# Window sums on another engine, key copies from another memory, and one step moved ahead, in a two-block transformer kernel

## The chip, the cores and the metric

The program runs on one core of a Trainium2 chip. Its time is device microseconds per execution; lower is better. The engines named here are TensorE (matrix products and transposes, called PE in the profile), VectorE (DVE), ScalarE (ACT), GpSimd (POOL) and SyncE (SP, whose queue issues the DMAs).

## The reference, cut to what matters

Two blocks of depth 2 follow each other on 512 tokens of width 1024, all in float32. The parts that the change touches are the multiscale pooling in both layers of the first block, the keys of the first mixer of the second block, and the latents of its second mixer.

```python
# block 1, both layers: window means of 2, 4, 8, 16 tokens (one window per 96 channels)
c = cs[:, :, g]                                   # running sum over tokens
prev = jnp.pad(c, ((0, 0), (w, 0), (0, 0)))[:, :s]
outs.append((c - prev) / cnt - ug[:, :, g])
pooled = jnp.stack(outs, axis=2)                  # then a small product per group

# block 2, layer 0: differential attention, 4 heads, two maps per head; and window attention
logits = [einsum('bqhmd,bkhmd->bmhqk', q, k) * scale for k, _ in kv_parts]   # 512 + 256 keys
outs = [einsum('bhqk,bkhd->bqhd', p[:, 0] - lam * p[:, 1], v) ...]

# block 2, layer 1: latent attention; one roped key of 32 features is shared by 16 heads
qn, qr = mla_queries(p[..., :C_Q_LORA], q_norm_g, wq_b)      # norm of 384 latents, product
kn, kr, v = mla_keys_values(p[..., C_Q_LORA:], kv_norm_g, wkv_b)
kr = apply_axial_rope(kr[:, :, None, :], tab)[:, :, 0, :]
```

## The kernel before

A float32 value is held as a high part, rounded to the matrix engine's reduced form, and a low part, the difference. `split` makes them: ScalarE copies the high part, VectorE subtracts. A product then takes three matrix products (`mm3`, lines 136 to 138): high by high, high by low, low by high. Weights arrive by DMA on SyncE's queue into three buffers, and `wload` splits them into five pairs of buffers.

**What sets the order.** The program is written as one sequence of instructions, and a planner in the compiler puts them into each engine's queue: it takes what its own model says is ready, earlier program lines first, and an engine then works through its queue strictly in order. Buffers are rings: a tile of a pool with n buffers waits until an earlier one is released.

**Attention and its filler.** In both attention stages of interest `pipeline` runs a list of items in four steps (scores with the maximum; exponential and scaling; transposes; product with the values). The steps of one item lie some items apart. After each round a `Fill` object runs generators that hold the next projections, up to an allowance in nanoseconds per item; a generator yields a cost figure for each piece, and a yield of 0.0 lets it stop early where little of the allowance is left. `need` runs what is left of a generator before the first item that uses it.

**Pooling** (`pool_in`, lines 579 to 605). It is filler in the first block's attention stage. For each of three chunks of 128 channels there is a projection of 8 x 3 products into a PSUM tile, a ScalarE copy to `u`, and then two, three or four doubling steps on GpSimd, each a small copy of the first columns (line 591) and one or two shifted additions (line 593). Two scalings at the window's start (line 599), two combined multiply-adds (lines 600 and 601) and a split follow on VectorE and ScalarE.

**Stacked keys** (`twice`, lines 1060 to 1074). The differential attention has ten items for each of four heads: eight for the tokens (four tiles by two maps) and two for the context. While one head's items run, `proj_ab` for the next group is the filler: six token tiles of 24 products and a rope, after the fifth tile the transposes of tiles 0 to 3, after the sixth those of the two context tiles. Keys of two maps come out of one transpose, 64 partitions each. For each map a tile of 128 partitions holds the high and low parts on its own 64 partitions and the same values again on the other 64:

```python
for h, k in enumerate(dsts):
    own, other = slice(64 * h, 64 * h + 64), slice(64 - 64 * h, 128 - 64 * h)
    self.split(k[own, 0, c], k[own, 1, c], ps[own])
    self.copy(k[other, 0, c], ps[own])
    self.copy(k[other, 1, c], f32(k[own, 1, c]))
```

`ps` is one of two PSUM tiles with the tag "p" that the projections and the value products use too (for the first group, which runs ahead of the items, the tags are "p" and "T"). `stacked` (lines 1044 to 1058) does the queries in a similar way, without copies.

**Latents** (`mla_latents`, lines 1413 to 1455). It projects key and value latents (288 columns) for six token tiles, then query latents (384 columns) for four, each with a norm, transposes and a split. The shared roped key, 32 columns, is gathered in `krs`; six transposes (line 1450), two splits of 32 x 768 and four GpSimd copies (line 1454) put it into the keys of both head pairs. The PSUM ring "ps" is closed behind this function, and the attention stage opens its own pools in the same banks.

Of the kernel before, what the change touches and what calls it, by code (L numbers as in the profile page):

```python
# [17 lines left out]
ALU = mybir.AluOpType  # L18
# [14 lines left out]
def f32(ap):  # L33
    return ap.bitcast(F32)
# [5 lines left out]
class Fill:  # L40
# [28 lines left out]
    def drain(self):  # L69
        while self.gens:  # L70
            self._one()
# [7 lines left out]
class Net:  # L79
# [499 lines left out]
    def pool_in(self, l, hT, pooled):  # L579
        nc, I = self.nc, self.I  # L580
        for c in range(3):
            yield 0.0
            ps = self.psum("p")
            yield from self.projT_steps(ps, self.wload(I["w_pool"][l, c]), hT)
            new = lambda: self.t2.tile([P, 4, P], F32, name="t2")
            u = new()
            self.copy(u, ps.rearrange("p (b j) -> p b j", b=4))
            cur, keep = u, []
            for i, k in enumerate((1, 2, 4, 8)[: c + 2]):
                nxt = new()  # L590
                nc.gpsimd.tensor_copy(self.heads(nxt, k), self.heads(cur, k))
                for (d, s), (d0, _) in zip(self.shifts(nxt, cur, k), self.shifts(cur, cur, k)):
                    nc.gpsimd.tensor_tensor(d, d0, s, op=ALU.add)  # L593
                cur = nxt
                keep.append(nxt)
            t = new()
            pc = self.poolc[:, c]
            for i, s in enumerate(keep[-2:]):
                nc.vector.tensor_tensor(s[:, :, 0:4], s[:, :, 0:4], pc[:, i, 1:17].rearrange("p (b j) -> p b j", b=4), op=ALU.mult)
            nc.vector.scalar_tensor_tensor(t, keep[-2], pc[:, 0, 0:1], u, op0=ALU.mult, op1=ALU.subtract)  # L600
            nc.vector.scalar_tensor_tensor(t, keep[-1], pc[:, 1, 0:1], t, op0=ALU.mult, op1=ALU.add)
            tt = self.qk.tile([P, 2, 512], R, name="qk")
            self.split(tt[:, 0], tt[:, 1], t.rearrange("p b j -> p (b j)"))
            pooled.append(tt)
# [455 lines left out]
    def twice(self, tok, col, tiles, dsts, tag):  # L1060

        tiles = list(tiles)
        n = len(tiles) * P
        yield 0.0
        ps = self.psum(tag)[:, :n]
        for j, t in enumerate(tiles):
            self.nc.tensor.transpose(ps[:, j * P : (j + 1) * P], tok[:, t, col : col + P], self.ident)
            yield 109
        c = slice(tiles[0] * P, tiles[0] * P + n)
        for h, k in enumerate(dsts):  # L1070
            own, other = slice(64 * h, 64 * h + 64), slice(64 - 64 * h, 128 - 64 * h)
            self.split(k[own, 0, c], k[own, 1, c], ps[own])
            self.copy(k[other, 0, c], ps[own])
            self.copy(k[other, 1, c], f32(k[own, 1, c]))

    def scores(self, ps, q, k):

# [212 lines left out]
    def mix_ab(self, hT, lead):  # L1290
        nc, I = self.nc, self.I
        with ExitStack() as ctx:
            with ExitStack() as c2:
                self.ringctx.close()
                self.psum_pools(c2, S=2, T=2, p=2)
                self.open_xc()
                hT = hT + self.new_hC()
                rows = []

                def pre(t):  # L1300
                    if not rows:
                        rows.extend((self.mod_row(0, 1, 1), self.mod_col(0, 1, 0)))
                    self.prenorm(self.xc[t - 4], rows[0], hT, t, rows[1])

                self.late += [(4, lambda: pre(4)), (5, lambda: pre(5))]
                cp = self.pool(c2, "const2")
                self.consts2(cp)
                self.tables(cp, ("cos_ab", "sin_ab"), 64)
                self.work = self.pool(c2, "attn")
                self.qk = self.pool(c2, "qk", 5)  # L1310
                fill = Fill(1500.0)
                gs = [{} for _ in range(6)]
                drain(self.proj_ab(hT, 0, gs[0], ("p", "T", "T")))
                self.xcctx.close()
                back = self.spill_x()
                self.qk2 = self.pool(c2, "qk2")
                self.ptp = self.pool(c2, "PT", 3)
                oBp = self.pool(c2, "oB")
                oB = [oBp.tile([P, 6, P], F32, name=f"oB{h}") for h in range(4)]
                proj = [(i, self.proj_ab(hT, i, gs[i], ("p",))) for i in range(1, 6)]  # L1320
                items = []
                for h in range(4):
                    items += self.diff_items(h, gs[h], fill, oB[h], proj[h])
                n, oT = len(items), []
                items += self.window_items(gs[4], gs[5], fill, oB, oT, proj[4])
                self.pipeline(items, fill, [3000] * n + [5000] * 8 + [200] * (len(items) - n - 8), (0, 1, 4, 5))
                fill.drain()
            self.open_x(back)
            self.open_xc()
            self.open_ring()  # L1330
            hT = self.b2_out(ctx, 0, oT, I["ab_w_out_2"], self.x + self.xc, lead)
        return hT
# [80 lines left out]
    def mla_latents(self, hT, lat, kTs):  # L1413

        nc, I = self.nc, self.I
        work = self.work
        gq = work.tile([P, 384], F32, name="gq")
        nc.sync.dma_start(gq, I["mla_q_norm_g_2"].rearrange("e d -> (e d)").partition_broadcast(P))
        gk = work.tile([P, 256], F32, name="gk")
        nc.sync.dma_start(gk, I["mla_kv_norm_g_2"].rearrange("e d -> (e d)").partition_broadcast(P))  # L1420
        qlT = (lat.tile([P, 3, 512], R, name="qlhi"), lat.tile([P, 3, 512], R, name="qllo"))
        klT = (lat.tile([P, 2, 768], R, name="klhi"), lat.tile([P, 2, 768], R, name="kllo"))
        krs = work.tile([P, 6, 96], F32, name="krs")
        nc.gpsimd.memset(krs, 0.0)

        def norm_T(src, n, g, dst, t):
            r = self.rstd(src, n)
            tok = work.tile([P, 384], F32, name="lat", bufs=2)[:, :n]
            nc.vector.scalar_tensor_tensor(tok, src, r, g, op0=ALU.mult, op1=ALU.mult)

            def tr():
                ps = self.psum()[:, 0]
                for c in range(n // P):
                    nc.tensor.transpose(ps[:, c * P : (c + 1) * P], tok[:, c * P : (c + 1) * P], self.ident)
                q = slice(t * P, (t + 1) * P)
                self.split(dst[0][:, :, q], dst[1][:, :, q], ps[:, :n].rearrange("p (c q) -> p c q", c=n // P))

            return tr

        def kv_evac(t, ps):  # L1440
            nc.vector.tensor_copy(krs[:, t, 64:96], ps[:, 256:288])
            if t < 4:
                self.rope2(krs[:, t : t + 1, 64:96], self.tabs["cos_c"][:, t], self.tabs["sin_c"][:, t], 1, 32)
            return norm_T(ps[:, :256], 256, gk, klT, t)

        drain(self.tok_proj(hT, I["mla_w_kv_2"], (4, 5, 0, 1, 2, 3), 288, kv_evac, tags=("ps",)))
        drain(self.tok_proj(hT, I["mla_w_q_2"], range(4), 384, lambda t, ps: norm_T(ps, 384, gq, qlT, t), tags=("ps",)))
        ps = self.psum().rearrange("p a b -> p (a b)")
        for t in range(6):
            nc.tensor.transpose(ps[:96, t * P : (t + 1) * P], krs[:, t], self.ident)  # L1450
        for j in range(2):
            self.split(kTs[j][0][64:96, 0], kTs[j][1][64:96, 0], ps[64:96, :768])
            for i in range(2):
                nc.gpsimd.tensor_scalar(kTs[j][i][64:96, 1], f32(kTs[j][i][64:96, 0]), 1.0, 1.0, op0=ALU.mult, op1=ALU.mult)
        return qlT, klT

    def proj_mla(self, grp, pr, qlT, klT, kT, g, tags):
# [316 lines left out]
```

## Time and profile before

| what | value |
|---|---|
| median of three timed runs | 3585.54 us (3582.1 to 3585.82) |
| the profiled execution: its own time, its span | 3584.89 us, 3583.1 us |
| TensorE, products | 3472.2 us busy, 97% |
| TensorE, weight loads (beside products) | 2966.2 us, 83% |
| VectorE | 1945.1 us, 54% |
| ScalarE | 1367.2 us, 38% |
| GpSimd | 411.1 us, 11% |
| mean granted TensorE clock | 0.989 |

The span runs from the first to the last instruction. Busy products are pipelined, so the 97% says that TensorE is rarely without work, not that it runs at its best rate. In a timeline each row has the start and the length in microseconds, the engine, the line, the operation and its tiles; in brackets stands how long the engine was idle before it and what it waited for.

### The profile page before, as it was taken

The page shows a single profiled execution, that of the slowest core. Times are in us where ns is not written, and L with a number is a line of the kernel's source. Part 1 is how long each engine was busy: PE and PEld are TensorE (multiplying, and loading weights), DVE is VectorE, ACT ScalarE, POOL GpSimd, SP SyncE. Part 2 cuts the span into 40 slices and gives each one's busy share as a digit, 9 for nine tenths or more (in the row PEclk, how much of TensorE's full clock was granted, in tenths as well). Part 3 has the DMA queues.
Part 4 walks back from the last instruction along what each step waited for, and adds up shares of the span by engine and source line. Part 5 has one row for each costly group of instructions (what it writes and reads, how often), then busy time and mean ns, then how long its engine had stood idle before and what let it go on. Part 6 is the DMA issues. An engine that isn't in the chain of part 4 may idle for free.

```text
span 3583.1 us, 48034 instructions
## 1 busy us (share of the span) xinstructions
PE 3472.2 (97%) x19101; PEld 2966.2 (83%) x19101; DVE 1945.1 (54%) x3140; ACT 1367.2 (38%) x2462; POOL 411.1 (11%) x532
## 2 busy tenths in 40 slices
PE   8999999999999999999999989999999989999998
PEld 8877798888897778988878887888888879888887
DVE  4453357466544435566767777536663466743243
ACT  4332344332443324532345556332111356643222
POOL 0201111000102111200010113200000122220001
PEclk9999999999999999999999999999999999999999
DMA  4243334344322433354331112325442121022232
GB/s 129 83 129 94 100 113 141 106 144 135 104 80 79 135 94 124 119 170 149 124 115 40 36 36 90 130 89 168 133 134 102 46 80 33 26 88 89 89 102 86
DMA packets 110129, 364.01 MB, mean 102 GB/s; under 512 B 16616, under 2 KB 18208, under 8 KB 109904
## 3 DMA queue, kind: packets, MB, share of 16 engines
q1 hardware_dynamic: 109904, 360.94, 31.8%
q8 instruction: 150, 2.46, 0.3%
q14 instruction: 75, 0.61, 0.1%
HBM read 347.16 MB, written 13.73 MB: 101 GB/s over the span
## 4 chain that ended last, share of the span: by engine, by line
PE 85%; DVE 5%; ACT 4%; POOL 2%; DMA 2%; issue 2%; SPq 0%; POOLq 0%; ACTq 0%; DVEq 0%
PE ps L136 21%; PE ps L137 21%; PE ps L138 21%; PE p L136 4%; PE p L137 4%; PE p L138 4%; PE p L456 2%; PE T L440 2%; DVE wlo L112 1%; PE S L1079 1%; DMA adaw<-in_ada_w_dram 1%; PE S L136 1%; POOL t L593 1%; PE p L1133 1%; ACT whi L109 1%
## 5 line engine op out<-in xcount | busy, mean ns | idle before, releaser
L112 DVE TENSOR_TENSOR wlo<-raw,whi 128x1024 fp32r<-128x1024 f32 (+2 forms) x510 | 604.2, 1189 | 740.1 <-ACT whi L109 720.1
L109 ACT ACTIVATE whi<-raw 128x1024 fp32r<-128x1024 f32 (+2 forms) x510 | 518.4, 1019 | 1152.7 <-PE ps L137 715.8
L137 PE MATMUL ps<-hTlo,whi 128*128 128x512 f32 (+1 forms) x2048 | 758.2, 370 | 4.3 <-DVE hTlo L184 3.4
L136 PE MATMUL ps<-hThi,whi 128*128 128x512 f32 (+1 forms) x2048 | 758.2, 371 | 2.7 <-ACT hThi L109 1.4
L138 PE MATMUL ps<-hThi,wlo 128*128 128x512 f32 (+1 forms) x2048 | 757.2, 370 | 0.0
L136 PEld LDWEIGHTS ps<-hThi,whi 128*128 128x128 f32 x2048 | 386.4, 189 | 73.2 <-issue 3.5
L137 PEld LDWEIGHTS ps<-hTlo,whi 128*128 128x128 f32 x2048 | 387.1, 189 | 69.6 <-DVE hTlo L184 3.9
L138 PEld LDWEIGHTS ps<-hThi,wlo 128*128 128x128 f32 x2048 | 386.9, 189 | 65.8
L945 DVE SCALAR_TENSOR_TENSOR acc<-adaw,cs,acc 128x1024 f32<-128x1024 f32 x168 | 209.6, 1280 | 12.5 <-DMA adaw<-in_ada_w_dram 12.3
L136 PE MATMUL ps<-whi,a 128*128 128x512 f32 x440 | 170.8, 392 | 0.5 <-ACT a L109 0.5
L138 PE MATMUL ps<-whi,a 128*128 128x512 f32 x440 | 170.6, 390 | 0.0
L137 PE MATMUL ps<-wlo,a 128*128 128x512 f32 x440 | 170.6, 390 | 0.0
L136 PE MATMUL p<-whi,hThi 128*128 128x384 f32 x464 | 161.2, 348 | 5.8 <-ACT hThi L182 3.1
L137 PE MATMUL p<-wlo,hThi 128*128 128x384 f32 x464 | 157.4, 339 | 4.0 <-DVE wlo L112 4.0
L138 PE MATMUL p<-whi,hTlo 128*128 128x384 f32 x464 | 157.5, 340 | 1.1 <-DVE hTlo L112 1.1
L269 DVE TENSOR_TENSOR y<-y,ps 128x1024 f32<-128x1024 f32 x88 | 106.6, 1218 | 85.9 <-PE ps L138 85.6
L161 POOL TENSOR_SCALAR rstd<-ms 128x1 f32<-128x1 f32 x54 | 18.5, 343 | 1073.7 <-ACT junk L159 1059.5
L136 PE MATMUL ps<-whi,act 128*128 128x512 f32 x352 | 138.1, 394 | 0.0
L137 PE MATMUL ps<-wlo,act 128*128 128x512 f32 x352 | 137.4, 392 | 0.0
L138 PE MATMUL ps<-whi,act 128*128 128x512 f32 x352 | 136.2, 390 | 0.0
L430 POOL TENSOR_SCALAR g<-g,den 128x768 f32<-128x768 f32 (+3 forms) x88 | 72.7, 828 | 478.0 <-DVE den L426 414.9
L409 DVE TENSOR_REDUCE nm<-S 128x1 f32<-128x768 f32 x96 | 91.4, 952 | 30.4 <-PE S L138 18.9
(439 smaller groups left out, 6731.3 us busy)
## 6 DMA issues: line engine op xcount, KB each, us to landing
raw<-in_ffn_w_dram SPq DMA_DIRECT2D x132, 512.0 KB
adaw<-in_ada_w_dram SPq DMA_DIRECT2D x96, 512.0 KB
raw<-in_w_up_dram SPq DMA_DIRECT2D x88, 512.0 KB
raw<-in_w_gate_dram SPq DMA_DIRECT2D x48, 512.0 KB
raw<-in_w_down_dram SPq DMA_DIRECT2D x44, 512.0 KB
raw<-in_w_qkv_dram SPq DMA_DIRECT2D x48, 384.0 KB
xd<-x SPq DMA_DIRECT2D x20, 512.0 KB
raw<-in_w_conv_dram SPq DMA_DIRECT2D x18, 512.0 KB
```

The source lines that it names most:

```text
L109: return self.nc.scalar.activation(out, in_, AF.Copy, scale=scale)
L112: return self.nc.vector.tensor_tensor(out, a, b, op=ALU.subtract)
L136: mm(ps, lhsT=l[0], rhs=r[0], start=first, stop=False)
L137: mm(ps, lhsT=l[0], rhs=r[1], start=False, stop=False)
L138: mm(ps, lhsT=l[1], rhs=r[0], start=False, stop=last)
L269: self.nc.vector.tensor_tensor(yps[t], yps[t], y, op=ALU.add)
L409: self.nc.vector.tensor_reduce(nm, sv, axis=AX.X, op=ALU.min)
L430: self.nc.gpsimd.tensor_scalar(Pt, Pt, r, 1.0, op0=ALU.mult, op1=ALU.mult)
L440: nc.tensor.transpose(ps[:, k * P : (k + 1) * P], Pt[:, (k0 + k) * P : (k0 + k + 1) * P], self.ident)
L456: self.nc.tensor.matmul(o[64 * h : 64 * h + 64], lhsT=vs(h, k), rhs=PTs[h][:, k], start=k == ks[0], stop=k == ks[-1])
L593: nc.gpsimd.tensor_tensor(d, d0, s, op=ALU.add)
L945: nc.vector.scalar_tensor_tensor(acc[r], w, c, acc[r], op0=ALU.mult, op1=ALU.add)
```

## The change

In `pool_in` the doubling steps run on VectorE instead of GpSimd. In `twice` both splits are made first, and then each map's other half is one copy of high and low together from SBUF, on ScalarE for the first map and on GpSimd for the second. The filler allowance in the differential items goes from 3000 to 3600. In `mla_latents` the queries' latents come after the shared roped key instead of before it.

```diff
@@ pool_in
-                nc.gpsimd.tensor_copy(self.heads(nxt, k), self.heads(cur, k))
+                nc.vector.tensor_copy(self.heads(nxt, k), self.heads(cur, k))
                 for (d, s), (d0, _) in zip(self.shifts(nxt, cur, k), self.shifts(cur, cur, k)):
-                    nc.gpsimd.tensor_tensor(d, d0, s, op=ALU.add)
+                    nc.vector.tensor_tensor(d, d0, s, op=ALU.add)
@@ twice
             self.split(k[own, 0, c], k[own, 1, c], ps[own])
-            self.copy(k[other, 0, c], ps[own])
-            self.copy(k[other, 1, c], f32(k[own, 1, c]))
+        for h, k in enumerate(dsts):
+            own, other = slice(64 * h, 64 * h + 64), slice(64 - 64 * h, 128 - 64 * h)
+            if h:
+                self.nc.gpsimd.tensor_copy(k[other, :, c], f32(k[own, :, c]))
+            else:
+                self.copy(k[other, :, c], f32(k[own, :, c]))
@@ mix_ab
-                self.pipeline(items, fill, [3000] * n + [5000] * 8 + [200] * (len(items) - n - 8), (0, 1, 4, 5))
+                self.pipeline(items, fill, [3600] * n + [5000] * 8 + [200] * (len(items) - n - 8), (0, 1, 4, 5))
@@ mla_latents
         drain(self.tok_proj(hT, I["mla_w_kv_2"], (4, 5, 0, 1, 2, 3), 288, kv_evac, tags=("ps",)))
-        drain(self.tok_proj(hT, I["mla_w_q_2"], range(4), 384, lambda t, ps: norm_T(ps, 384, gq, qlT, t), tags=("ps",)))
         ps = self.psum().rearrange("p a b -> p (a b)")
...
+        drain(self.tok_proj(hT, I["mla_w_q_2"], range(4), 384, lambda t, ps: norm_T(ps, 384, gq, qlT, t), tags=("ps",)))
         return qlT, klT
```

## Rows read from the trace of the kernel before

**Rows 1.** The page's first table, TensorE and the others: busy us, share, instructions.
```profile
PE 3472.2 (97%) x19101; PEld 2966.2 (83%) x19101; DVE 1945.1 (54%) x3140; ACT 1367.2 (38%) x2462; POOL 411.1 (11%) x532
```

**Rows 2.** Busy time by stretch; after the engines granted clock, DMA share, GB/s.
```profile
145.00:165.00 20.00, 17.17 (x101) 13.62 (x100) 9.09 (x16) 7.58 (x13) 6.83 (x10) 0.91 0.32 102
175.00:205.00 30.00, 25.50 (x155) 20.25 (x156) 15.07 (x29) 9.08 (x16) 5.21 (x8) 0.94 0.25 77
...
1930.00:1960.00 30.00, 25.61 (x155) 23.25 (x154) 20.07 (x44) 19.98 (x52) 2.75 (x4) 0.94 0.18 53
```

**Rows 3.** Timeline of GpSimd, third pooling chunk of the first layer.
```profile
172.44 0.76 POOL L591 COPY t<-t 128x1 f32<-128x1 f32 x1 [4.01 <-ACT t L109]
...
176.04 0.20 POOL L591 COPY t<-t 128x4 f32<-128x4 f32 x1
```

**Rows 4.** Timeline of VectorE, the same chunk.
```profile
171.93 1.23 DVE L112 TENSOR_TENSOR wlo<-raw,whi 128x1024 fp32r<-128x1024 f32 x1 [0.26 <-ACT whi L109]
...
178.49 0.26 DVE L599 TENSOR_TENSOR t<-t,poolc 128x16 f32<-128x16 f32 x2 [5.34 <-POOL t L593]
...
181.36 0.96 DVE L411 CUSTOM_DVE_ANT_0 S<-S,mask 128x768 f32<-128x768 f32 x1
```

**Rows 5.** Timeline of TensorE behind the first and the third chunk.
```profile
155.98 0.30 PE L440 MATMUL T<-ident,yg 128*128 128x128 f32 x1 [2.25 <-ACT PT L109]
...
183.84 0.55 PE L440 MATMUL T<-ident,g 128*128 128x128 f32 x3 [4.50 <-ACT PT L109]
...
185.19 0.63 PE L136 MATMUL p<-hThi,whi 128*128 128x512 f32 x1
...
188.32 0.39 PE L138 MATMUL p<-hThi,wlo 128*128 128x512 f32 x1
```

**Rows 6.** Timeline of VectorE: two-input operations of 512, 1 and 128 columns.
```profile
155.49 0.69 DVE L112 TENSOR_TENSOR qk<-t,qk 128x512 fp32r<-128x512 f32 x1 [0.69 <-ACT qk L109]
...
1978.90 0.16 DVE L1125 TENSOR_TENSOR den<-den,nlam 128x1 f32<-128x1 f32 x1
...
1979.19 0.28 DVE L1022 TENSOR_TENSOR ropeA<-tok,cos_ab 128x128 f32<-128x128 f32 x1
```

**Rows 7.** Timeline of TensorE at a head change of the differential attention.
```profile
1987.00 0.82 PE L440 MATMUL T<-ident,g 128*128 128x128 f32 x6
1990.32 0.88 PE L440 MATMUL T<-ident,big 128*128 128x128 f32 x3 [2.50 <-DVE big L1126]
...
1992.12 0.69 PE L136 MATMUL p<-whi,hChi 128*128 128x384 f32 x1
```

**Rows 8.** Timeline of ScalarE at the same head change.
```profile
1986.26 0.58 ACT L109 ACTIVATE qb<-p 64x512 fp32r<-64x512 f32 x1
...
1988.21 0.59 ACT L109 ACTIVATE qb<-p 64x512 fp32r<-64x512 f32 x1
...
1991.48 0.59 ACT L109 ACTIVATE qc<-p 64x512 fp32r<-64x512 f32 x1
```

**Rows 9.** Timeline of VectorE at the same head change.
```profile
1987.07 0.67 DVE L112 TENSOR_TENSOR qb<-p,qb 64x512 fp32r<-64x512 f32 x1
...
1990.20 0.69 DVE L112 TENSOR_TENSOR qc<-p,qc 64x512 fp32r<-64x512 f32 x1
```

**Rows 10.** Timeline of TensorE at the end of the first group's projection.
```profile
1900.21 0.44 PE L136 MATMUL T<-whi,hChi 128*128 128x384 f32 x1 [2.59 <-ACT qc L109]
```

**Rows 11.** Timeline of GpSimd and of VectorE, both at 1914 us.
```profile
1913.86 0.91 POOL L430 TENSOR_SCALAR big<-big,den 128x768 f32<-128x768 f32 x1 [28.14 <-DVE den L426]
...
1914.07 0.83 DVE L1022 TENSOR_TENSOR ropeA<-tok,cos_ab 128x128 f32<-128x128 f32 x1
```

**Rows 12.** Timeline of VectorE and of TensorE at the end of the latents.
```profile
2920.36 0.56 DVE L112 TENSOR_TENSOR qllo<-ps,qlhi 128x384 fp32r<-128x384 f32 x1 [0.23 <-ACT qlhi L109]
...
2923.24 0.95 DVE L112 TENSOR_TENSOR kTlo<-ps,kThi 32x768 fp32r<-32x768 f32 x1 [0.87 <-ACT kThi L109]
...
2924.34 0.66 PE L136 MATMUL p<-whi,qlhi 128*128 128x384 f32 x1 [3.88 <-DVE kTlo L112]
```

## The prediction, made before the changed kernel was run

> **What bounds the kernel now.** I read the page's first table, then the busy time by stretch, then the timelines of single engines where the change lies. TensorE is busy 97% of the span [rows 1], so a gain can come only from places where it waits, or where its clock is down. The stretches show three such kinds of place, and the diff touches each. From 175 to 205 us (pooling, first layer) it is busy 25.50 of 30 us, and the granted clock is 0.94; from 145 to 165 us 17.17 of 20 at 0.91; in a head change of the second mixer, 1930 to 1960 us, 25.61 of 30 at 0.94 [rows 2]. The clock has a price of its own: one minus the mean times the length, 30 x 0.06 or 20 x 0.09, is 1.8 us of lost work in each of the three. It is the step from 2.4 to 1.2 GHz that follows a long wait: after an idle of 4.50 us a product of 512 columns takes 0.63 us, three us later 0.39 [rows 5]. A removed wait of over 2 us is thus worth its length and up to 1.8 us more.
>
> **Pooling sums.** For each of three 128-channel chunks GpSimd makes two, three or four window sums, one from the other. The third chunk's chain starts at 172.44 us and its first two steps end at 176.04 [rows 3]; all four end where VectorE stops waiting for it, at 178.49 [rows 4]. So two steps take 3.60 us, four 6.05. VectorE stands still for the last 5.34 of them, because the scaling (L599) is next in its queue. Behind it wait a weight split and the maxima of the next attention item, at 181.36 [rows 4]; ScalarE's exponentials and probability copies wait for those, and TensorE's transposes for the copies: idle 4.50 us before 183.84, and in the first chunk 2.25 before 155.98 [rows 5]. The second chunk has no such wait.
>
> On VectorE the same operations cost: a sum over 512 columns 0.69, over 128 columns 0.28, over one 0.16 [rows 6]. In a straight line between 128 and 512, 384 columns are 0.55 and 256 are 0.41. Two steps are copy 0.16, sums of 384 and 127 columns 0.55 + 0.28, copy 0.16, two sums of 256 and 254 columns 0.82: 1.97. Steps three and four, each a copy and a sum of some 506 columns, add 0.85 each: 3.67 for four. VectorE is in a weight split when the chunk arrives and is free at 173.16, 0.72 later than GpSimd was [rows 3, 4]. So the chains end 3.60 - 1.97 - 0.72 = 0.9 us sooner in the first chunk and 6.05 - 3.67 - 0.72 = 1.66 sooner in the third. Nothing is displaced: VectorE was idle in that time. The waits shrink by as much, to 1.35 and 2.84. After 2.84 us I let the clock fall as before; after 1.35 I count half of the 1.8 as saved, since the shortest wait after which my rows show it fallen is 2.25. Per layer 0.9 + 0.9 + 1.66 = 3.5; both layers have the same stretch, so **-6.9 us**. Bounds: 0 if another instruction takes the place of the wait, and -20.7 if both waits go with their clock (6.75 + 3.6, twice).
>
> **Stacked keys.** In each head change the key's transposes lie in one of two PSUM tiles "p"; each of the two maps gets a high half (ScalarE), a low half (VectorE), and two copies to the other 64 partitions (ScalarE), the first of them from PSUM. ScalarE does the first high half at 1986.26, a first PSUM copy at 1988.21 and the last at 1991.48, ending at 1992.07 [rows 8]. There TensorE's next projection tile, which needs that PSUM tile, begins: 1992.12 [rows 7]. Until then TensorE had no other work ready: it ended its transposes at 1987.82, waited 2.50 us for VectorE's mix of the two maps, and ran slow afterwards (0.69 for 384 columns) [rows 7].
>
> After the change PSUM is read only by the two high halves and two subtractions. The first subtraction runs at 1987.07 and ends at 1987.74, the second, 0.69 long, was last in line at 1990.20 [rows 9]. Directly behind the first it ends at 1988.43, with a query's split between them at 1989.1. The projection tile can then fill the wait, which falls from 2.50 to between 0.6 and 1.3: -1.6, and with it the clock, -1.8. That is 3.4 for each of four head changes; the first group, where the same tile waits 2.59 for the same copy [rows 10], gives 3.4 too: -17.0. ScalarE loses four copies of 0.59 and gains one of twice the length, which runs beside TensorE's tile.
>
> Against it stand two additions. GpSimd copies the second map's key: 1024 columns at the rate of its 128x768 scaling in 0.91 [rows 11] are an estimated 1.21 us, and 0.6 for the two context tiles. It holds back no scores, since the second map comes an item later; but while GpSimd ran its 0.91, VectorE's rotation of 128 columns took 0.83 instead of 0.28 [rows 6, 11]. The cost is between 0 and 1.21 per head; I take 0.4. The Trainium skill, "SBUF — State Buffer", section "SBUF: two separate sides", says that the port pair which the two engines share is an exclusive lock: a VectorE instruction with two SBUF inputs and a GpSimd one that reads SBUF don't overlap at all. By that rule the cost is the whole copy, and the trace's 0.83 agrees with it.
>
> The fill allowance of 3600 instead of 3000 ns per item brings the burst from item 7 to item 5 by the generator's own cost figures, and the context tiles' from item 8 to item 7. Items 8 and 9 then have no projection behind them. That can cost from nothing (the planner brings the next group's tile forward) to one more wait as in rows 7 with its clock, 4.3; I take 1.2, half a wait without the clock. Together 1.6 for each of four heads: +6.4. The sum is **-10.6 us**.
>
> **Latents.** The roped key is now the last use of the old PSUM ring: its second low half runs from 2923.24 to 2924.19, and the first product of the attention pools starts behind it at 2924.34, after 3.88 us of idle [rows 12]. Moved ahead, the last use is the queries' low half, 2920.36 + 0.56 = 2920.92 [rows 12]: 3.4 us sooner. The six transposes move too and now lie in a stretch where TensorE works; six take 0.82 [rows 7]. The splits (two on each of ScalarE and VectorE) and four GpSimd copies lie beside the queries' projection, where these engines mostly wait for TensorE. The clock after the wait: half of 1.8. Together -3.4 + 0.8 - 0.9 = **-3.5 us**, bounds 0 and -5.2.
>
> **Sum.** -6.9 - 10.6 - 3.5 = -21.0. The profiled execution took 3584.9 us (span 3583.1 and 1.8 around it), 0.6 below the median of the runs shown. Forecast: **3564 us**.
>
> **Rivals.**
> 1. *The waits go altogether in the pooling.* The order on each engine is the planner's; with the chain on VectorE the maxima may run between its steps, as they are ready before the third chain ends. Then -20.7 replaces -6.9, and the head changes reach -17.0: 3585 - 41 = 3544. For: VectorE has room. Against: program order puts the chain first.
> 2. *The head change keeps its loss.* The PSUM tile is free sooner, but items 8 and 9 starve, or the GpSimd copies lock VectorE where its queue is full. Rows 7 speak for it: TensorE was waiting for VectorE, not for PSUM. Then only -6.9 and -3.5 remain: 3574. With the locks alone at full price, five copies of 1.21 and five of 0.6 instead of 1.6 counted, the loss is 7.5: 3572.
> 3. *No gain.* The sums' and latents' time goes into the next wait of the same queue, as the weight split before the maxima shows it can: 3585.
> 4. *Slower.* The larger allowance empties the last three items of a head (7, 8, 9), and each gets a wait like rows 7 with its clock: 12.9 per head instead of 4.3, four times, +34.4; the first group, sums and latents give back 13.8: 3605. It decides the sign from an added 5.3 us per head. For: the present wait stands just where little projection is left. Against: three items lie between softmax and transposes, so a short chain is covered.
>
> **How the numbers follow.** Chances: forecast (3553 to 3572) 0.45, rival 1 0.13, rival 2 0.20, rival 3 0.12, rival 4 0.10. Faster by over 0.2% (7.2 us, about what separates a change from none here) are the first three: 0.78; within it 0.12; slower 0.10. The range leaves out the far end of rival 1 and rival 4: 3543 to 3584.
>
> **What would show it.** Pooling: VectorE's idle before L599 gone, a wait under 3 us where 4.50 stood, one clock dip per layer. Keys: the projection tile starts within about 1 us of the transposes, no dip at the head changes, a GpSimd copy of 64 x 1024. Latents: the first attention product within 1.5 us of the last transposes. The prediction is wrong if head changes lose as much as before, or if new waits stand at items 7 to 9.

## The result, and the profile after

The changed kernel takes 3548.55 us in the median of three runs (3546.56 to 3548.8) where the kernel before, timed beside it, takes 3585.68: a ratio of 0.9897, 95% interval 0.9877 to 0.9916, so about 37 us less. (A fourth run, 3929.17 us at a granted clock of 0.823, was disturbed and is no part of the comparison.) The forecast was 3564, with 3543 to 3584 as its range. The sign and all three places were right; the gain is some 1.75 times the forecast of 21. The time lies in the range, but below the band of 3553 to 3572 to which the prediction gave its 0.45.

Where the 36.4 us of span went (3583.1 to 3546.7) is read from four landmarks in TensorE's timeline that both kernels have: the end of the first block, the end of the attention in the second block's first mixer (the differential attention, which the prediction calls the second mixer), the start of the second block's latents, and the first score product of the latent attention. First the kernel before, then the changed one; the columns are those of the timelines ahead of the prediction.

```profile
1875.72 1.03 PE L176 MATMUL S<-ident,big 128*128 128x128 f32 x8
...
2223.99 0.50 PE L136 MATMUL ps<-whi,hChi 128*128 128x512 f32 x1 [0.93 <-DVE hClo L112]
...
2861.45 1.07 PE L176 MATMUL ps<-ident,big 128*128 128x128 f32 x8 [0.90 <-DVE y L269]
...
2940.44 0.50 PE L136 MATMUL S<-kThi,hChi 96*128 96x512 f32 x1 [0.68 <-ACT hChi L109]
```

```profile
1856.63 1.04 PE L176 MATMUL S<-ident,big 128*128 128x128 f32 x8
...
2190.29 0.50 PE L136 MATMUL ps<-whi,hChi 128*128 128x512 f32 x1 [0.93 <-DVE hClo L112]
...
2826.49 1.06 PE L176 MATMUL ps<-ident,big 128*128 128x128 f32 x8 [0.91 <-DVE y L269]
...
2903.65 0.50 PE L136 MATMUL S<-kThi,hChi 96*128 96x512 f32 x1 [0.68 <-ACT hChi L109]
```

Subtracting gives five stretches. I, up to the first landmark (pooling): 1875.72 to 1856.63, **-19.1**. II (stacked keys): 348.27 to 333.66, **-14.6**. III, untouched: -1.3. IV (latents): 78.99 to 77.16, **-1.8**. V, untouched: +0.4. The sum is -36.4.

**Pooling.** TensorE's stretches, answering to [rows 2]: the clock is 1.00 in all three, and it is busy 29.44 of 30 us where it was 25.50.

```profile
145.00:165.00 20.00, 19.24 (x115) 15.48 (x115) 14.38 (x34) 8.48 (x14) 1.79 (x2) 1.00 0.40 131
175.00:205.00 30.00, 29.44 (x176) 23.96 (x173) 14.19 (x29) 10.57 (x20) 3.65 (x4) 1.00 0.20 57
1910.00:1940.00 30.00, 27.80 (x182) 25.69 (x181) 23.64 (x57) 18.59 (x50) 6.87 (x7) 1.00 0.18 53
```

TensorE's timeline behind the first and the third chunk, against [rows 5]: 2.25 has become 0.76, and 4.50 is gone, since the row at 175.99 waits for nothing.

```profile
154.59 0.52 PE L440 MATMUL T<-ident,yg 128*128 128x128 f32 x3 [0.76 <-ACT PT L109]
...
175.99 0.55 PE L440 MATMUL T<-ident,g 128*128 128x128 f32 x3
```

VectorE, third chunk, against [rows 4]. The chain runs from 167.03 to 170.15: 3.1 us for four steps, below the 3.67 I had priced. It is over three microseconds before the maximum (L411), which waits only for its scores.

```profile
167.03 0.15 DVE L591 COPY t<-t 128x1 f32<-128x1 f32 x1
...
169.47 0.68 DVE L593 TENSOR_TENSOR t<-t 128x504 f32<-128x504 f32 x1
170.18 0.26 DVE L599 TENSOR_TENSOR t<-t,poolc 128x16 f32<-128x16 f32 x2
...
173.20 0.97 DVE L411 CUSTOM_DVE_ANT_0 S<-S,mask 128x768 f32<-128x768 f32 x1 [0.25 <-PE S L509]
```

The chain did not only get shorter, it starts 5.4 us earlier than GpSimd's at 172.44 [rows 3]. Of this, 3.3 us were saved before the second chunk: its copy out of PSUM moved from 163.00 to 159.72. ScalarE's timeline tells the rest. In the kernel before, the second chunk's split stood at the head of ScalarE's queue and waited 6.74 us for the second chunk's sums; the third chunk's copy out of PSUM was queued behind it, at 171.80, which is 8.80 us behind the second chunk's copy (first row).

```profile
163.00 0.58 ACT L109 ACTIVATE t<-p 128x512 f32<-128x512 f32 x1
...
170.31 0.63 ACT L109 ACTIVATE qk<-t 128x512 fp32r<-128x512 f32 x1 [6.74 <-DVE t L601]
...
171.80 0.57 ACT L109 ACTIVATE t<-p 128x512 f32<-128x512 f32 x1
```

In the changed kernel the same two instructions run one after the other, without a wait, and the two copies lie 5.96 us apart:

```profile
159.72 0.58 ACT L109 ACTIVATE t<-p 128x512 f32<-128x512 f32 x1
...
165.16 0.61 ACT L109 ACTIVATE qk<-t 128x512 fp32r<-128x512 f32 x1
165.68 0.58 ACT L109 ACTIVATE t<-p 128x512 f32<-128x512 f32 x1
```

**Stacked keys.** One head by busy time, from a score product of one head to the same product of the next, before and after. The head is 2.56 us shorter. Waiting is only 0.86 of that (50.32 - 45.94 = 4.38 against 47.76 - 44.24 = 3.52); the other 1.70 is the same work done faster, and 0.03 of clock over 50.32 us is 1.5.

```profile
1936.44:1986.76 50.32, 45.94 (x283) 43.21 (x281) 35.17 (x97) 27.54 (x76) 6.27 (x8) 0.97 0.11 32
```

```profile
1923.68:1971.44 47.76, 44.24 (x280) 41.43 (x280) 35.92 (x97) 24.53 (x69) 9.31 (x10) 1.00 0.11 33
```

TensorE's waits in that head, all that the timeline shows, against the 2.50 of [rows 7], which stands once in each head change: one long wait and five of up to 0.58 have become four of less than 1 us.

```profile
1956.95 0.73 PE L1083 MATMUL S<-qc,qa 128*128 128x512 f32 x2 [0.71 <-ACT yg L421]
1958.66 0.66 PE L1052 MATMUL p<-ident,tok 128*128 128x128 f32 x4 [0.98 <-DVE v L1093]
...
1960.93 1.58 PE L1137 MATMUL p<-v,PT 128*128 128x128 f32 x12 [0.71 <-DVE qc L112]
...
1971.44 0.50 PE L1083 MATMUL S<-qb,qa 128*128 128x256 f32 x2 [0.95 <-ACT qb L109]
```

In the first group the wait of 2.59 [rows 10] is 1.47, and the clock around it (1860 to 1890 us) is 1.00. Over the whole of II, TensorE waits 5.1 us less (26.6 for 31.7) and does its work in 9.5 us less (307.1 for 316.6): most of this gain is faster work.

**Latents.** The wait of 3.88 [rows 12] is 1.17, but the clock still falls behind it and the 1.88 before it: 0.34 for a product of 384 columns, then 0.51 and 0.52 for 3 us. The six transposes stand at 2864.42 and take 0.96.

```profile
2886.33 0.55 PE L1438 MATMUL ps<-ident,lat 128*128 128x128 f32 x3 [1.88 <-DVE lat L1433]
...
2888.05 0.44 PE L136 MATMUL p<-whi,qlhi 128*128 128x384 f32 x1 [1.17 <-DVE qllo L112]
...
2888.50 0.34 PE L138 MATMUL p<-whi,qllo 128*128 128x384 f32 x1
...
2888.85 0.51 PE L137 MATMUL p<-wlo,qlhi 128*128 128x384 f32 x1
```

### The profile page after: what moved, and what is told of

It reads as the page before. It is cut to its first block, busy times and chain, and to the rows that moved or that the text cites. A ratio compares the mean times of both kernels' runs of the same rounds, so it can differ in the third digit from the quotient of the medians.

```text
span 3546.7 us, 48008 instructions
## 1 busy us (share of the span) xinstructions
PE 3456.6 (97%) x19101; PEld 2953.9 (83%) x19101; DVE 1959.7 (55%) x3188; ACT 1353.0 (38%) x2432; POOL 395.6 (11%) x494
## 3 DMA queue, kind: packets, MB, share of 16 engines
q8 instruction: 150, 2.46, 0.3%
## 4 chain that ended last, share of the span: by engine, by line
PE 87%; DVE 5%; ACT 3%; DMA 2%; POOL 1%; issue 1%; SPq 0%; POOLq 0%; ACTq 0%; DVEq 0%
PE ps L136 21%; PE ps L138 21%; PE ps L137 21%; PE p L136 4%; PE p L137 4%; PE p L138 4%; PE p L456 3%; PE T L440 2%; PE S L1083 1%; DMA adaw<-in_ada_w_dram 1%; DVE wlo L112 1%; PE S L136 1%; PE p L1137 1%; PE S L138 1%; PE S L137 1%
## 5 line engine op out<-in xcount | busy, mean ns | idle before, releaser
L109 ACT ACTIVATE PT<-T 128x384 f32<-128x384 f32 (+2 forms) x160 | 73.8, 461 | 87.6 <-PE T L440 84.1
```

The lines of the kernel that those rows point to most:

```text
L109: return self.nc.scalar.activation(out, in_, AF.Copy, scale=scale)
```

## The experiments

All twelve in one table. "I", "II" and "IV" are the stretches named above, in us, from one profile of each kernel. The ratio is to the kernel before, timed on the same chip, with its 95% interval.

| kernel | ratio | I | II | IV |
|---|---|---|---|---|
| before | 1 | 1875.7 | 348.3 | 79.0 |
| changed | 0.9897 [0.9877, 0.9916] | 1856.6 | 333.7 | 77.2 |
| e1_pool | 0.9947 [0.9932, 0.9961] | 1855.2 | 349.6 | 78.8 |
| e2_keys | 0.9968 [0.9956, 0.9980] | 1875.8 | 335.8 | 79.1 |
| e3_fill | 1.0009 [1.0000, 1.0019] | 1875.1 | 351.8 | 77.9 |
| e4_rope | 0.9988 [0.9979, 0.9998] | 1878.1 | 347.5 | 76.0 |
| e8_mid_only | 0.9968 [0.9956, 0.9979] | 1865.5 | 348.9 | 77.5 |
| e6_mid_pool | 0.9912 [0.9895, 0.9928] | 1861.5 | 333.2 | 75.8 |
| e5_no_fill | 0.9902 [0.9887, 0.9917] | 1857.9 | 336.0 | 77.1 |
| e7_both_act | 0.9912 [0.9897, 0.9926] | 1859.9 | 338.6 | 74.4 |
| x1_psum_src | 0.9955 [0.9940, 0.9970] | 1855.5 | 353.8 | 75.3 |
| f_4500 | 0.9892 [0.9876, 0.9909] | 1857.6 | 330.9 | 76.1 |
| f_6000 | 0.9920 [0.9905, 0.9935] | 1855.3 | 340.3 | 75.2 |
| w_8000 | 0.9899 [0.9884, 0.9914] | 1858.9 | 331.3 | 76.0 |

A stretch is not the same in all profiles of the same code. III, which no kernel edits, goes from 635.3 to 639.9. I goes from 1875.1 to 1878.1 in the four kernels with the pooling of before and from 1855.2 to 1859.9 in the eight with the new; II goes from 347.5 to 349.6 in the four with the old keys and allowance. So differences of under some 5 us in I, and under some 2 or 3 in II, are told by single rows or not at all.

### The pooling sums alone

```diff
-                nc.gpsimd.tensor_copy(...)   # line 591; the same in line 593
+                nc.vector.tensor_copy(...)
```

> The kernel before with the pooling sums on VectorE and nothing else. Theory M (both waits and their clock falls go, in each layer): the end of the first block comes 18 to 20 us sooner, and the whole kernel takes 3565 to 3568 us. The prediction's theory P (each wait only shortens by what VectorE is faster): 6.9 us sooner, 3578. Third, the gain seen in the changed kernel came partly from elsewhere: between 7 and 15 sooner.

I is 20.5 us shorter, and the ratio is 19.0 us; the means of I over the eight and the four kernels named above differ by 19.1. Theory M holds, the prediction's 6.9 does not.

### The second chunk alone, from both sides

e8_mid_only is the kernel before with only the second chunk on VectorE; e6_mid_pool is the changed kernel with only the second chunk on GpSimd.

```diff
+                eng = nc.vector if c == 1 else nc.gpsimd    # e8; the reverse in e6
-                nc.gpsimd.tensor_copy(...)
+                eng.tensor_copy(...)
```

> The kernel before with only the second chunk's window sums on VectorE; the first and the third stay on GpSimd. Theory H (before, ScalarE stood 6.74 us behind the second chunk's split, which waited for GpSimd's chain, so that the third chunk was copied out of PSUM at 171.80 and not at 165.7; it is this delay, not the third chain's own length, that stood in front of the maxima): the third chunk's chain starts about 5 us sooner, ends near 173 us, before or about when the next scores exist, and the idle of 4.50 falls below 1.5 with its clock. The first chunk keeps its 2.25. 4.5 + 1.8 per layer less what stays: 8 to 13 us sooner at the end of the first block, 3573 to 3578. Theory P (the prediction's: the second chunk has no wait, so its engine doesn't matter): within 1 us of before.

> The changed kernel with only the second chunk's window sums back on GpSimd. Theory H: ScalarE stands behind the second split again, the third chunk starts some 6 us later, and though its chain is on VectorE (3.2 us), TensorE waits again, by the prediction's own working 4.50 - 1.66 = 2.8 us, with a clock fall of 1.8: 4.6 per layer, 9 us, 3556 to 3559. Theory P: within 1 us of the changed kernel, 3549.

e8 moves the one chunk that has no wait of its own and gains 10.2 us in I, half of the whole. ScalarE copies the third chunk 5.97 us behind the second where it was 8.80, so 2.83 sooner, and the wait behind the third chunk, whose own chain is still on GpSimd, falls by nearly as much, 2.89, from 4.50 to 1.61. The wait of the first chunk stays. ScalarE, then TensorE, first layer:

```profile
163.91 0.58 ACT L109 ACTIVATE t<-p 128x512 f32<-128x512 f32 x1
...
169.88 0.58 ACT L109 ACTIVATE t<-p 128x512 f32<-128x512 f32 x1
```

```profile
157.80 0.52 PE L440 MATMUL T<-ident,yg 128*128 128x128 f32 x3 [2.46 <-ACT PT L109]
...
181.87 0.55 PE L440 MATMUL T<-ident,g 128*128 128x128 f32 x3 [1.61 <-ACT PT L109]
```

By stretches of e8_mid_only the clock is 1.00 in both, where it was 0.91 and 0.94 [rows 2]:

```profile
145.00:165.00 20.00, 16.65 (x104) 13.24 (x103) 9.34 (x17) 7.58 (x13) 5.49 (x8) 1.00 0.39 126
175.00:205.00 30.00, 27.90 (x182) 22.16 (x181) 17.04 (x34) 11.18 (x21) 4.94 (x7) 1.00 0.24 69
```

With its clock the third chunk gives 2.89 + 1.8 = 4.7 of the 5.1 per layer. The clock behind the first chunk stayed up too, though its wait did not shrink; that is worth 1.8 per layer by the same price, and no edit accounts for it. So the third chunk's own 2 x 4.7 = 9.4 is the surer figure. In e6_mid_pool ScalarE stands behind the second split again (its timeline, first row), and TensorE waits behind a third chunk whose chain is on VectorE (its timeline, second fence):

```profile
167.01 0.63 ACT L109 ACTIVATE qk<-t 128x512 fp32r<-128x512 f32 x1 [6.75 <-DVE t L602]
```

```profile
178.20 0.55 PE L440 MATMUL T<-ident,g 128*128 128x128 f32 x3 [2.17 <-ACT PT L109]
```

I is 4.9 us longer than in the changed kernel, about what that stretch varies by itself, and the timed intervals overlap; but the wait of 2.17 stands in both layers, which makes 4.3. I had expected 9: the wait came (2.17 for 2.84), the clock fall did not (1.00 from 175 to 205 us). Theory H is shown from both sides in its cause, by these rows; its price in e6 is smaller, and not clear of the noise by the times.

### The stacked keys alone, and the allowance alone

```diff
# e2_keys: only the edit in twice; the allowance stays
# e3_fill: only this
-  [3000] * n + ...
+  [3600] * n + ...
```

> The kernel before with the new order and copies of the stacked keys, the filler allowance left at 3000. Theory A (copies from SBUF free the PSUM tile, which is the whole gain): the stretch from the end of the first block to the first S product of the latent attention's predecessor stage shrinks by 12 to 15 us, the whole to 3570 to 3574. Theory B (the larger allowance carries much of it, because burst and softmax no longer meet): 4 to 8 us, the rest with the allowance. The prediction's terms: 17.0 less 1.6 for the locks, 15.4.

> The kernel before with the filler allowance 3600 instead of 3000 and nothing else. Theory A (the allowance alone is no gain, the PSUM copies still hold the tile): within 3 us of before. Theory B: 4 to 10 us faster, since the burst then lies two items earlier, where VectorE and ScalarE have fewer items behind them. The prediction's term: 4.8 us slower, from starved items at the end of each head.

The copies alone shorten II by 12.4, the allowance alone lengthens it by 3.5. So theory A for the copies, and for the allowance a loss near the prediction's 4.8 in size (timed, 1.0009 with an interval from 1.0000 to 1.0019, it is at the edge of what can be told). That items starve at the end of a head is not shown as its cause: the waits of 0.70 and 0.98 in a head of e3_fill stand in the changed kernel as well (0.71 and 0.98), and those that the changed kernel lacks are 1.77 before transposes that wait for ScalarE's probability copy and 1.03 before value products that wait for a key copy.

### The allowance taken back, and made larger

```diff
# e5_no_fill: 3000, f_4500: 4500, f_6000: 6000
-  [3600] * n + ...
+  [3000] * n + ...
# w_8000
-  [5000] * 8
+  [8000] * 8
```

> The changed kernel with the filler allowance back at 3000. If the parts add up, as measured alone (the allowance alone made the second mixer's stretch 3.5 us longer): 3 us faster, 3545 to 3546. If the allowance works only together with the new copies (with the copies alone the stretch is 12.4 us shorter, with both 14.6): 2 us slower, 3550 to 3552. The waits at the head changes and in front of the window items tell which.

> The changed kernel with a filler allowance of 4500. Rival 4 of the prediction (a larger allowance starves the last items of a head): waits like the one before the window items (2.5 to 2.9 with a clock fall) appear at each head's end, 4 heads of 4.3 us: 3566. If the planner brings the next head's work forward anyway: within 3 us of the changed kernel, 3546 to 3552.

> The changed kernel with a filler allowance of 6000, at which the projection ends half-way through a head. Rival 4: over 17 us slower, 3566 or more. Otherwise: within 4 us of the changed kernel; the sign is open.

> The changed kernel with the allowance of the eight window items at 8000 instead of 5000. The largest waits left in the second mixer, 2.49 and 2.89 us with a clock of 0.70 between them, stand in front of the window items and at the first of them. If more projection early in the window stage can be laid there, up to 5.4 of waits and 3 of clock go: 3541 to 3547. If the planner can't move it ahead of the first window item, the waits stay and the end of the window stage starves instead: 3548 to 3553.

Without the larger allowance II is 2.3 us longer: with the new copies the allowance is no loss any more, perhaps a small gain (by the timed ratios, 0.9902 and 0.9897, it can't be told from nothing). At 3000 each head keeps one wait of 2.30, which takes the clock along in three of the four heads, as this row of e5_no_fill shows (0.66 for 384 columns); at 3600 there are the four short ones.

```profile
1965.51 0.66 PE L136 MATMUL p<-whi,hChi 128*128 128x384 f32 x1 [2.30 <-DVE qc L112]
```

At 4500 II is 2.8 us shorter than at 3600, at 6000 6.6 longer. At 4500 the largest waits in a head are 1.55 and 1.26, so no head ends with the waits of 2.5 to 2.9 that rival 4 needs, and even 6000 costs less than the 4 x 5.3 from which rival 4 decides. (6000 is outside the 4 us that I had given it, by its ratio some 8.) With the longer window allowance the waits of 2.49 and 2.89 are gone, with 1.26 and 1.39 as the largest in their place, and II is 2.4 shorter; the timed runs don't show it. By the ratios neither 4500 (0.9892) nor the window allowance (0.9899) differs from the changed kernel (0.9897). The two together were not run.

### What in the new copies does it

e7_both_act makes both copies from SBUF on ScalarE; x1_psum_src keeps the new order of the splits but copies the high part from PSUM again.

```diff
# e7_both_act
-            if h:
-                self.nc.gpsimd.tensor_copy(k[other, :, c], f32(k[own, :, c]))
-            else:
-                self.copy(k[other, :, c], f32(k[own, :, c]))
+            self.copy(k[other, :, c], f32(k[own, :, c]))
# x1_psum_src, in the same place
+            self.copy(k[other, 0, c], ps[own])
+            self.copy(k[other, 1, c], f32(k[own, 1, c]))
```

> The changed kernel with both copies of the stacked keys on ScalarE, none on GpSimd. Theory L (GpSimd's copy of 1.03 us holds VectorE's two-input operations, as 0.95 instead of 0.28 us for a rotation beside another GpSimd instruction, and that reaches the path): 0.4 per group sooner, 1.5 to 3 us in the second mixer. Theory S (ScalarE's queue is the one that scores and transposes wait for, its new copy of 1.04 delays them): 1 us per head later, 4 in all. Third, both lie beside other work: within 1 us.

> The changed kernel, in which the stacked keys keep the new order (both splits first), but each map's other half is made as before: ScalarE copies the high part from PSUM and the low part from SBUF, 64 x 512 each. Theory A (the gain of 14.6 us is the release of the PSUM tile before the copies): the tile is held by two to three copies of 0.59 again, TensorE waits 1.2 to 1.8 longer per group of keys, and up to 1.8 of clock with it where the wait passes 2 us: 5 to 15 us more, 3554 to 3564. Theory O (the order of the splits and the queue of ScalarE are the whole gain): no more than both copies from SBUF on ScalarE cost, 5 us in that stretch, 3554.

With PSUM as the source II is 353.8, no better than the allowance alone (351.8): the order of the splits by itself gives nothing. The value products, which need the PSUM tile, wait for the copy out of it, once per head, with 2.35 to 2.45 us. From x1_psum_src, ScalarE and then TensorE:

```profile
1980.50 0.38 ACT L109 ACTIVATE qc<-p 64x256 fp32r<-64x256 f32 x1
```

```profile
1980.94 1.60 PE L1135 MATMUL p<-v,PT 128*128 128x128 f32 x12 [2.45 <-ACT qc L109]
```

Reading SBUF instead, still on ScalarE, gives 353.8 - 338.6 = 15.2 us; the second copy on GpSimd another 338.6 - 333.7 = 4.9. The two kernels of the first difference also differ in the number of copies: ScalarE is busy 210.1 us of II with four smaller ones and 205.3 with two. Since taking 9.1 us off ScalarE (205.3 to 196.2) gave those 4.9, an estimated 2 to 3 us of the 15.2 may be ScalarE's time and not the PSUM tile; no run parts them. So theory A, with 20 us (353.8 - 333.7) above the 15 that I had set as its end; and theory S against theory L: taking the GpSimd copy away costs, it doesn't give. In e7 a head takes 49.16 us where it takes 47.76 in the changed kernel, and the value products wait 1.48, in each of the four heads, where the changed kernel has nothing over 0.98 in the head shown above:

```profile
1977.23 1.58 PE L1134 MATMUL p<-v,PT 128*128 128x128 f32 x12 [1.48 <-DVE qc L112]
```

### The latents alone

```diff
-        drain(self.tok_proj(hT, I["mla_w_q_2"], ...))   # ahead of the roped key
+        drain(self.tok_proj(hT, I["mla_w_q_2"], ...))   # behind it
```

> The kernel before with the shared roped key made ahead of the queries' latents and nothing else. The changed kernel's trace says -1.8 us in the stretch up to the first S product of the latent attention (wait 2.7 shorter, about 1 of transposes more, the clock falls still). The prediction's term is -3.5, with half of a clock fall saved. If the two other changes had a part in it, the stretch here differs from -1.8 by over 0.5.

IV is 3.0 us shorter, and the timed ratio is 4.3 us with an interval from 0.7 to 7.5. More is told by all profiles together: IV has a mean of 78.5 in the five kernels without the move (77.5 to 79.1) and of 75.9 in the nine with it (74.4 to 77.2). That is -2.6.

## Why the prediction was right in sign and short in size

**Pooling: 6.9 forecast, 19.1 measured.** The steps "Nothing is displaced" and "VectorE was idle in that time" held, and the price of four steps was 0.55 too high (3.12 for 3.67). What failed is the sentence "The second chunk has no such wait". It has none on TensorE, but its split holds ScalarE for 6.74 us, and in ScalarE's queue stands the third chunk's copy. My 1.66 us for the third chunk counted from a start that I took as given; counted from the second chunk's copy, the third's came 2.84 us sooner. Each part is seen alone: the chain on VectorE takes 2.33 off the wait (e6, 4.50 to 2.17), the freed ScalarE 2.89 (e8, 4.50 to 1.61). Together they are more than the 4.50 that there was, so the wait went altogether, and its clock fall with it. In the changed kernel the waits and clock falls sum to (2.25 - 0.76) + 4.50 + 2 x 1.8 = 9.6 per layer, 19.2 for both (in the second layer 0.98 remains for 0.76). Rival 1 had this size (20.7) by another mechanism: the maxima did not run between the steps of the third chain, the chain was over before their scores existed.

**Stacked keys: 10.6 forecast, 14.6 measured.** "PSUM is read only by the two high halves and two subtractions" is the main cause, as the return to PSUM shows. The wait was mis-sized. "The wait falls from 2.50 to between 0.6 and 1.3" counted on the second subtraction running "directly behind the first". In e2_keys it starts 2.2 us behind it (VectorE, below), since a query's subtraction and a maximum stand between them, and the wait stays at 2.30, with the clock fallen in three of the four heads. At 3600 the largest wait is 0.98, but there are four, and the waiting in the head fell by 0.86, not by 1.6. The clock's share of 1.8 per head came (1.70 of faster work in the head shown), and the first group's wait fell by 1.1 with its clock.

```profile
1980.42 0.67 DVE L112 TENSOR_TENSOR qb<-p,qb 64x512 fp32r<-64x512 f32 x1
...
1982.64 0.69 DVE L112 TENSOR_TENSOR qc<-p,qc 64x512 fp32r<-64x512 f32 x1
```

The copies alone gave 12.4 of the 15.4 (17.0 less 1.6 for the locks) that I had counted for them. Wrong in sign was the term for "starved head end", +4.8: the allowance alone does lose 3.5, but with the new copies it does not (-2.3, within the noise). The first error makes the forecast gain too large by 3 us, the second too small by some 7; that their sum is off by only 4 is luck.

**The locks**, +1.6 in the sum, don't show on the path: whatever the GpSimd copies cost, it is less than what they spare ScalarE, for without them the stretch is 4.9 us longer. By the Trainium skill, "SBUF — State Buffer", section "SBUF: two separate sides", a VectorE instruction with two SBUF inputs and a GpSimd one that reads SBUF exclude each other. That they exclude each other fits the rows in the last section. That TensorE pays for the whole copy, as the second case of rival 2 had it (3572), does not.

**Latents: 3.5 forecast, 2.6 measured** (the mean of all profiles; 1.8 between the two kernels' own). The wait fell by 2.71 where 3.4 was counted, and the transposes cost 0.96 where 0.8 was counted. The half clock fall did not come back.

The total of 3548.55 is nearer to rival 1's 3544 than to the forecast, and not for rival 1's reason. Rival 3 (no gain) and rival 2 (the head change keeps its loss) fall with the stretches; rival 4 falls with the changed kernel itself, whose four waits stay below 1 us in the head shown, and with the 4500 and 6000 kernels.

## What to carry to other kernels

Before pricing a slow instruction by the wait that it causes directly, follow what stands behind its consumers in every in-order queue: here half of the pooling gain lay in a chunk that no TensorE wait named, since its consumer blocked ScalarE's copy of the next chunk. Where a matrix engine waits for a PSUM tile, take from PSUM only what must come from there and make further copies from SBUF. A filler allowance is to be tuned again after such an edit: its loss of 3.5 us alone was gone with the new copies.

## What the runs showed of the hardware

**The same wait may or may not cost the clock.** At the end of the first block TensorE waits twice in every kernel, by 3.07 us and then by 1.40 to 3.24. In the kernel before the first wait is followed by a product at 0.66 and the second by one at 0.45:

```profile
1864.23 0.66 PE L136 MATMUL p<-whi,hThi 128*128 128x384 f32 x1 [3.07 <-ACT hThi L182]
...
1872.14 0.45 PE L137 MATMUL p<-wlo,hThi 128*128 128x384 f32 x1 [2.92 <-DVE wlo L112]
...
1874.16 0.33 PE L136 MATMUL T<-whi,hThi 128*128 128x384 f32 x1
```

In e4_rope, which has the same code up to there, the clock falls behind both. Behind the first wait the fall comes one row later, at 1864.44; behind the second the products run at 0.52 until 1877.31:

```profile
1863.75 0.41 PE L136 MATMUL p<-whi,hThi 128*128 128x384 f32 x1 [3.07 <-ACT hThi L182]
...
1864.44 0.52 PE L136 MATMUL p<-whi,hThi 128*128 128x384 f32 x1
...
1871.70 0.69 PE L137 MATMUL p<-wlo,hThi 128*128 128x384 f32 x1 [2.85 <-DVE wlo L112]
...
1877.31 0.52 PE L136 MATMUL T<-whi,hThi 128*128 128x384 f32 x1
```

From the second wait to the landmark the one takes 3.58 us (1872.14 to 1875.72) and the other 6.40 (1871.70 to 1878.10). Up to the second wait they are alike (7.91 and 7.95 us from the first). III varies by 4.6 (635.3 to 639.9) between kernels that don't differ there. The longest second wait, 3.24 us in e5_no_fill, is followed by a product at 0.44, so the length alone does not decide it. A wait of 2.46 us in e8_mid_only left the clock at 1.00, while in the latents it fell behind 1.88 and 1.17. A clock fall is thus to be priced as a chance, not as a sure 1.8.

**GpSimd can be the one that waits.** In the changed kernel its copy of 64 x 1024 takes 1.03, beside VectorE reading PSUM; its copy of half the size takes 1.38, started 0.02 us after a VectorE subtraction of two SBUF tiles (spans on GpSimd are rough, but a longer time for half the elements is more than that). GpSimd, then VectorE:

```profile
1960.92 1.03 POOL L1076 CAST qc<-qc 64x1024 fp32r<-64x1024 f32 x1 [6.65 <-DVE qc L112]
...
1971.58 1.38 POOL L1076 CAST qc<-qc 64x512 fp32r<-64x512 f32 x1 [4.43 <-DVE qc L112]
```

```profile
1971.56 0.94 DVE L112 TENSOR_TENSOR wlo<-raw,whi 128x768 fp32r<-128x768 f32 x1
...
1974.57 0.95 DVE L112 TENSOR_TENSOR wlo<-raw,whi 128x768 fp32r<-128x768 f32 x1
```

The subtraction beside it takes 0.94, no longer than the next one at 1974.57, which has no GpSimd instruction beside it: the one that came second paid, as VectorE did in [rows 11]. Two more cases go the same way: in e2_keys the copy of 64x1024 takes 1.81 (at 1983.46, 0.10 behind a VectorE operation on SBUF tiles), and in the changed kernel a scaling of 128x256 takes 1.25 at 1965.89, 0.05 behind one, and 0.48 at 1973.06.
